# Output norm of the difference attention: factors in one go, applied where the output projection reads its rows

## Chip, cores and metric

The kernel runs on one core of a Trainium2 chip, as one launch. The metric is the device time of a launch in microseconds (us); lower is better. The engines are named PE (TensorE), DVE (VectorE), ACT (ScalarE), POOL (GpSimd) and SP (SyncE, which issues the DMAs).

## What is computed

A transformer layer (difference attention and dilated attention side by side, then a gated output) and a second layer with sliding-window attention, on 2048 tokens of width 1024 in float32. The part that matters here:

```python
dq, dk, dv, bq, bk, bv, z = jnp.split(u, IN_SPLIT_IDX, axis=-1)
...
a = diff_attention(dq, dk, dv, lam, diff_slopes)      # (B, S, 4 heads, 128)
a = rms_norm(a, diff_sub_norm_g[i]) * (1.0 - lam_init)
a = a.reshape(B, S, DIFF_WIDTH)
...
b = dilated_attention(bq, bk, bv, dil_slopes).reshape(B, S, DIL_WIDTH)
y = jnp.concatenate([a, b], axis=-1) * jax.nn.silu(z)
x = x + y @ w_out[i]
```

The norm runs over the 128 columns of one head. So each row of each head has one factor, `1 / sqrt(mean(a * a) + eps)`: 2048 tokens times 4 heads, 8192 factors in all.

## The kernel before

Six stages follow one another in the trace, called A, B1, B2, C, D and E here after the functions. They overlap a little, since a scheduler sets the order of the instructions on each engine from a simulated timeline.

- **A** (0 to 773 us): input projection. It leaves queries, keys, values and `silu(z)` (`sz`) in DRAM.
- **B1** (`phase_b1`, 769 to about 1460 us): difference attention. A step `g` is one head `h` and one tile of 128 queries: 64 steps. Each step has two softmaxes (`e`) of two halves (`hf`) of 1024 keys. `scores` puts a half on PE (4 matmuls, L322); one DVE instruction (L328) evicts it from PSUM, adds the position bias and takes the maximum. `exps` is ACT's (L338). `combine` works out `cc` on DVE (L344, L346) and lets POOL subtract the second softmax from the first (L355, L356). `transposes` (PE L366, ACT L367, DVE L368) and `pv` (PE L380 to L382) follow some steps later.
- `finish` (L390 on) closes a pair of steps. It transposes the output back (L405), ACT divides by the softmax sum (L406) and sums the squares into `ssq` (L408). After every second pair it has four query tiles of a head. Then `rsqrt_dve` (L233) turns the four sums per row into factors: 13 DVE instructions on tiles of 128x4, each of which needs the one before. POOL multiplies the rows by `sz` times gain (L411), ACT scales each of the four tiles by its factor (L413), and SP stores them to `scr["y"][0]` (L414). That is 16 times in B1.
- **B2** (`phase_b2`): dilated attention. POOL splits transposed weights there (L586, L587) and merges the patterns (L659 to L678).
- **C** (`phase_c`): for each of 16 token tiles, `load_y` reads the rows of `y` (L806, 512 columns of the difference attention; L807 and L811, the rest), `product` transposes them (L797) and multiplies by `w_out`. The tile of L806 comes from the pool `c_y0` of one buffer, so the next load waits until PE has transposed the last one. The weights are split into high and low parts on POOL and DVE (L755).
- **D**, **E**: the second layer.

The factor loop, and the code that calls it:

```python
for step in range(3):
    nc.vector.tensor_mul(a, y, y)
    nc.vector.tensor_mul(a, a, v)
    if step < 2:
        nc.vector.scalar_tensor_tensor(y, a, (3.0, 12.0)[step], y, ALU.subtract, ALU.mult)
...
if half == 1:
    rs = rsqrt_dve(nc, fp, ssq, 128)
    nc.gpsimd.tensor_mul(an, an, szt)
    for t in range(4):
        nc.scalar.activation(an[:, t], an[:, t], AF.Copy, scale=rs[:, t:t + 1])
```

Of the kernel before, what the change touches and what calls it, by code (L numbers as in the profile page):

```python
# [7 lines left out]
F32 = mybir.dt.float32  # L8
F32R = mybir.dt.float32r
I32 = mybir.dt.int32  # L10
AF = mybir.ActivationFunctionType
# [5 lines left out]
P = 128  # L17
# [5 lines left out]


def rsqrt_mean(nc, c, pool, ss, n, out=None):
    """1 / sqrt(ss / n + eps), refined by one Newton step."""
    w = ss.shape[-1]
    sd = pool.tile([P, w], F32, name="rm_sd")
    nc.scalar.activation(sd, ss, AF.Sqrt, bias=c["eps"], scale=1.0 / n)
    v = pool.tile([P, w], F32, name="rm_v")  # L30
    nc.vector.tensor_scalar(v, ss, 1.0 / n, EPS, ALU.mult, ALU.add)
    nc.vector.reciprocal(sd, sd)
    nc.vector.tensor_mul(v, v, sd)
    nc.vector.tensor_mul(v, v, sd)
    nc.vector.tensor_scalar(v, v, -0.5, 1.5, ALU.mult, ALU.add)
    if out is None:
        out = pool.tile([P, w], F32, name="rm_o")
    nc.vector.tensor_mul(out, sd, v)
    return out
# [191 lines left out]


def rsqrt_dve(nc, pool, ss, n, out=None):  # L233
    """1 / sqrt(ss / n + eps) on VectorE alone: exponent-halving start, three Newton steps (the
    first leaves -2 y, the second 16 y, and the third takes the factor out)."""
    w = ss.shape[-1]
    v = pool.tile([P, w], F32, name="rd_v")
    nc.vector.tensor_scalar(v, ss, 1.0 / n, EPS, ALU.mult, ALU.add)
    sh = pool.tile([P, w], I32, name="rd_i")
    nc.vector.tensor_scalar(sh, v.bitcast(I32), 1, None, ALU.logical_shift_right)  # L240
    y = pool.tile([P, w], F32, name="rd_y")
    nc.vector.tensor_scalar(y.bitcast(I32), sh, -1.0, float(0x5F3759DF), ALU.mult, ALU.add)
    a = pool.tile([P, w], F32, name="rd_a")
    if out is None:
        out = y
    for step in range(3):
        if w == 1:
            nc.vector.tensor_scalar(a, v, y, y, ALU.mult, ALU.mult)
        else:
# [4 lines that stand above are left out]
        else:  # L254
            nc.vector.tensor_scalar(a, a, -0.5 / 4096, 1.5 / 16, ALU.mult, ALU.add)
            nc.vector.tensor_mul(out, y, a)
    return out


def phase_b1(tc, c, scr, ndist, sub_g, lam):  # L260
    nc = tc.nc
    NQ = 4 * NT
    with (
# [11 lines left out]
        tc.tile_pool(name="b_v", bufs=5) as vp,  # L275
        tc.tile_pool(name="b_p", bufs=6) as pp,
        tc.tile_pool(name="b_o", bufs=2) as op,
        tc.tile_pool(name="b_f", bufs=8) as fp,
        tc.tile_pool(name="b_pt", bufs=3, space=PSUM) as ps_t,
        tc.tile_pool(name="b_po", bufs=1, space=PSUM) as ps_o,  # L280
        tc.tile_pool(name="b_ps", bufs=2, space=PSUM) as ps_s,
# [102 lines left out]
        def evacuate(p):  # L384
            ot = op.tile([P, 256], F32, name="b_ot")
            nc.scalar.activation(ot, outs.pop(p), AF.Copy)
            outs[p, "t"] = ot

        def finish(p):
            h, pr = divmod(p, 8)  # L390
            b, half = divmod(pr, 2)
            if half == 0:
                outs["an"] = op.tile([P, 4, 128], F32, name="b_an")
                outs["ssq"] = fp.tile([P, 4], F32, name="b_ssq", bufs=2)
                szt = op.tile([P, 4, 128], F32, name="b_sz")
                nc.sync.dma_start(
                    szt, scr["sz"][b * 512:(b + 1) * 512, h * 128:(h + 1) * 128].rearrange("(t p) w -> p t w", p=P))
                nc.gpsimd.tensor_mul(szt, szt, g08.unsqueeze(1).broadcast_to([P, 4, 128]))
                outs["sz"] = szt
            an, ssq, szt = outs["an"], outs["ssq"], outs["sz"]  # L400
            ot = outs.pop((p, "t"))
            pb = ps_t.tile([P, 4, P], F32, name="t_ps")
            for qi in range(2):
                t = 2 * half + qi
                nc.tensor.transpose(pb[:, qi], ot[:, qi * P:(qi + 1) * P], c["id"])  # L405
                nc.scalar.activation(an[:, t], pb[:, qi], AF.Copy, scale=st[2 * p + qi]["r0"])  # L406
                junk = op.tile([P, P], F32, name="b_j")
                nc.scalar.activation(junk, an[:, t], AF.Square, accum_out=ssq[:, t:t + 1])  # L408
            if half == 1:
                rs = rsqrt_dve(nc, fp, ssq, 128)  # L410
                nc.gpsimd.tensor_mul(an, an, szt)  # L411
                for t in range(4):
                    nc.scalar.activation(an[:, t], an[:, t], AF.Copy, scale=rs[:, t:t + 1])  # L413
                nc.sync.dma_start(  # L414
                    scr["y"][0][b * 512:(b + 1) * 512, h * 128:(h + 1) * 128].rearrange("(t p) w -> p t w", p=P), an)

# [4 lines left out]
        for g in range(NQ + LT + 5):  # L421
            h, qt = divmod(g, NT)
            if g < NQ and qt == 0:
                for j in range(4):
                    load_v(h, j)
            if g < NQ and qt % 4 == 1:
                ng = g + 3
                if ng < NQ:
                    load_q(ng // NT, (ng % NT) // 4)
            for s in range(4):  # L430
                e, hf = divmod(s, 2)
                if g < NQ:
                    with tc.high_priority(offset=AHEAD) if g < EARLY else nullcontext():
                        scores(g, e, hf)
                    if qt == NT - 1 and h < 3 and hf == 1:
                        for j in range(4):
                            load_k(h + 1, e, j)
                if 0 <= g - LT < NQ:
                    transposes(g - LT, s)
                p, half = divmod(g - LT - 2, 2)  # L440
                if 0 <= p < NQ // 2:
                    for kt in range(8 * half + 2 * s, 8 * half + 2 * s + 2):
                        pv(p, kt)
                if s == FIN and half == 0 and 0 <= p - 1 < NQ // 2:
                    finish(p - 1)
                if g < NQ and hf == 1:
                    with tc.high_priority(offset=AHEAD) if g < EARLY else nullcontext():
                        exps(g, e)
            if g < NQ:
                with tc.high_priority(offset=AHEAD) if g < EARLY else nullcontext():  # L450
                    combine(g)
            p, half = divmod(g - LT - 2, 2)
            if half == 1 and 0 <= p < NQ // 2:
                evacuate(p)


LB = 4
# [309 lines left out]
def phase_c(tc, c, scr, x, p, w_out, ple_g, w_gate, w_proj, norm_g):  # L767
    nc = tc.nc
    with (
# [20 lines left out]
            store[k, ch] = w  # L790

        def to_t(src_of, dst, cuts):
            """transpose 128-column pieces, cuts[i]:cuts[i + 1] at a time, and split them into dst[:, 0] and dst[:, 1]"""
            for b, m in zip(cuts, [e - b for b, e in zip(cuts, cuts[1:])]):
                ps = pt.tile([P, 4, P], F32, name="c_tp")
                for j in range(m):
# [6 lines left out]
        def load_y(t):  # L803
            rows = slice(t * P, (t + 1) * P)
            ys = [yp.tile([P, 512], F32, name="c_yn") for yp in (yp0, yp1)]
            nc.sync.dma_start(ys[0], scr["y"][0][rows])  # L806
            nc.sync.dma_start(ys[1][:, 0:384], scr["y"][1][rows])  # L807
            state["y", t] = ys

# [1 line left out]
            nc.sync.dma_start(state["y", t][1][:, 384:512], scr["y"][2][t * P:(t + 1) * P])  # L811

        def product(t, cuts):
            """y times wo, of the 128-column pieces from cuts[0] to cuts[-1]"""
            ys = state["y", t]
            if cuts[0] == 0:
                state["yt", t] = (ap_.tile([P, 2, KD, P], F32R, name="c_at"),
# [96 lines left out]


def prep_swa(tc, c, scr, table, onehot, sinks, pm):
    """Sink logits, and the position bias by distance, repeated by rows so that a pitch one short reads it as a
    Toeplitz tile. All in units of 1/8."""
    nc = tc.nc
    sk8 = c["const"].tile([P, 16], F32, name="e_sk")  # L920
    nc.sync.dma_start(sk8, sinks.broadcast_to([P, 16]))
# [310 lines left out]
def consts(tc, cp):  # L1232
# [3 lines left out]
    make_identity(nc, c["id"])  # L1236
    c["eps"] = cp.tile([P, 1], F32, name="eps")
    nc.vector.memset(c["eps"], EPS)
    c["qs_dq"] = cp.tile([P, 8], F32, name="qs_dq")
    c["qs_bq"] = cp.tile([P, 8], F32, name="qs_bq")  # L1240
    for h in range(8):
# [3 lines left out]


def diff_lambda(tc, c, lams):
    nc, cp = tc.nc, c["const"]
    lt = cp.tile([P, 4, 64], F32, name="lt")
    for i, ap in enumerate(lams):  # L1250
        nc.sync.dma_start(lt[:, i], ap.broadcast_to([P, 64]))
    pr = cp.tile([P, 2, 64], F32, name="lpr")
    for i in range(2):
        nc.vector.tensor_mul(pr[:, i], lt[:, 2 * i], lt[:, 2 * i + 1])
    s2 = cp.tile([P, 2], F32, name="ls2")
    nc.vector.reduce_sum(s2, pr, axis=AX.X)
    nc.scalar.activation(s2, s2, AF.Exp)
    c["lam"] = cp.tile([P, 1], F32, name="lam")
    nc.vector.tensor_sub(c["lam"], s2[:, 0:1], s2[:, 1:2])
    nc.vector.tensor_scalar(c["lam"], c["lam"], LAM_INIT, None, ALU.add)  # L1260


def tables():
# [65 lines left out]
```

## Time and profile before

| | |
|---|---|
| median of 3 runs | 3122.9 us (3122.07 to 3132.4) |
| profiled execution, first to last instruction | 3126.1 us |
| PE busy | 96% of the span |
| DVE / ACT / POOL busy | 63% / 51% / 37% |
| mean granted PE clock | 0.977 of full speed |
| DMA | 352.78 MB, 112 GB/s over the span |

The profile gives one execution, on the same single core. Of that execution only the span is known, 3.2 us over the median of the runs. "Busy" is the union of an engine's instructions; matmuls are pipelined. The idle time that stands before a group of instructions is put down to what released the engine last.

### The profile page before, as it was taken

The page shows a single profiled execution, that of the slowest core. Times are in us where ns is not written, and L with a number is a line of the kernel's source. Part 1 is how long each engine was busy: PE and PEld are TensorE (multiplying, and loading weights), DVE is VectorE, ACT ScalarE, POOL GpSimd, SP SyncE. Part 2 cuts the span into 40 slices and gives each one's busy share as a digit, 9 for nine tenths or more (in the row PEclk, how much of TensorE's full clock was granted, in tenths as well). Part 3 has the DMA queues.
Part 4 walks back from the last instruction along what each step waited for, and adds up shares of the span by engine and source line. Part 5 has one row for each costly group of instructions (what it writes and reads, how often), then busy time and mean ns, then how long its engine had stood idle before and what let it go on. Part 6 is the DMA issues. An engine that isn't in the chain of part 4 may idle for free.

```text
span 3126.1 us, 45716 instructions
## 1 busy us (share of the span) xinstructions
PE 2988.1 (96%) x15778; PEld 2499.6 (80%) x15778; DVE 1980.9 (63%) x4986; ACT 1591.5 (51%) x3528; POOL 1165.9 (37%) x1052
## 2 busy tenths in 40 slices
PE   8999999999988888988999989999999999999998
PEld 7788888887877777777887867888888888888787
DVE  4215555423999999997787765444445666666765
ACT  5223233312877666776877753222235666666621
POOL 1110011110876667763454540000035565555421
PEclk9999999999999999998999999999999999999999
DMA  7654444415131211106757563233273424232452
GB/s 211 126 132 102 104 118 118 111 61 174 30 91 39 81 55 48 54 15 154 173 143 163 123 167 112 88 107 105 89 238 97 155 88 155 88 116 80 130 190 84
DMA packets 421928, 352.78 MB, mean 113 GB/s; under 512 B 104480, under 2 KB 367168, under 8 KB 418624
## 3 DMA queue, kind: packets, MB, share of 16 engines
q1 hardware_dynamic: 421552, 348.83, 39.8%
q8 instruction: 126, 2.06, 0.3%
q0 software_dynamic: 144, 1.02, 0.2%
q14 instruction: 106, 0.87, 0.1%
HBM read 234.26 MB, written 116.52 MB: 112 GB/s over the span
## 4 chain that ended last, share of the span: by engine, by line
PE 80%; DVE 11%; DMA 4%; issue 2%; ACT 2%; SPq 1%; POOL 0%; DVEq 0%; ACTq 0%; POOLq 0%
PE psm L181 7%; PE psm L183 7%; PE psm L182 7%; PE e_mm L762 5%; PE e_mm L764 5%; PE s_ps L322 5%; PE e_mm L763 4%; PE c_mm L762 4%; PE c_mm L763 4%; PE c_mm L764 4%; DVE et L328 4%; PE d_sr L564 4%; PE t_ps L366 2%; PE f_mm L762 2%; PE f_mm L763 2%
## 5 line engine op out<-in xcount | busy, mean ns | idle before, releaser
L181 PE MATMUL psm<-w,hh 128*128 128x512 f32 x1024 | 406.3, 398 | 9.9 <-DVE t L111 7.1
L183 PE MATMUL psm<-w,hh 128*128 128x512 f32 x1024 | 399.5, 393 | 0.0
L182 PE MATMUL psm<-w,hl 128*128 128x512 f32 x1024 | 399.3, 391 | 0.0
L982 POOL TENSOR_TENSOR e_wt<-e_raw,e_wt 128x1024 fp32r<-128x1024 f32 x80 | 191.3, 2398 | 478.1 <-DMA e_raw<-in_a_w_in_dram 403.9
L322 PE MATMUL s_ps<-kst,qst 128*128 128x512 f32 x1024 | 309.3, 429 | 55.2 <-DVE mx L328 54.6
L101 POOL TENSOR_TENSOR w<-wraw,w 128x512 fp32r<-128x512 f32 x64 | 81.6, 1297 | 599.6 <-ACT w L100 589.6
L356 POOL TENSOR_TENSOR et<-et 128x1024 f32<-128x1024 f32 x124 | 295.1, 2401 | 0.0
L322 PEld LDWEIGHTS s_ps<-kst,qst 128*128 128x128 f32 x1024 | 187.3, 202 | 103.7 <-DVE mx L328 77.1
L338 ACT ACTIVATE et<-et,nm 128x2048 f32<-128x2048 f32 x128 | 257.0, 2007 | 5.7
L181 PEld LDWEIGHTS psm<-w,hh 128*128 128x128 f32 x1024 | 193.3, 189 | 48.5 <-DVE t L111 7.5
L762 PE MATMUL e_mm<-e_x,e_wt 128*128 128x512 f32 x576 | 228.1, 396 | 1.3 <-DVE e_k L1024 0.9
L764 PE MATMUL e_mm<-e_x,e_wt 128*128 128x512 f32 x576 | 226.8, 394 | 0.0
L763 PE MATMUL e_mm<-e_x,e_wt 128*128 128x512 f32 x576 | 226.6, 393 | 0.0
L183 PEld LDWEIGHTS psm<-w,hh 128*128 128x128 f32 x1024 | 192.9, 189 | 41.1
L182 PEld LDWEIGHTS psm<-w,hl 128*128 128x128 f32 x1024 | 193.7, 189 | 38.3
L355 POOL TENSOR_SCALAR et<-et,cc 128x1024 f32<-128x1024 f32 x124 | 138.4, 1131 | 215.8 <-DVE cc L346 122.9
L366 PE MATMUL t_ps<-id,et 128*128 128x128 f32 x1024 | 163.2, 289 | 21.0 <-DVE ptl L368 19.8
L1070 DVE CUSTOM_DVE_ANT_0 e_es<-e_s,e_bias,e_sk 128x256 f32<-128x256 f32 (+1 forms) x256 | 117.3, 472 | 104.1 <-PE e_s L1062 73.5
L1083 POOL TENSOR_SCALAR e_es<-e_es,e_l 128x256 f32<-128x256 f32 (+1 forms) x256 | 119.6, 488 | 170.2 <-DVE e_l L1081 105.2
L367 ACT ACTIVATE pth<-t_ps 128x512 fp32r<-128x512 f32 x256 | 146.4, 590 | 62.8 <-PE t_ps L366 57.7
L368 DVE TENSOR_TENSOR ptl<-t_ps,pth 128x512 fp32r<-128x512 f32 x256 | 170.5, 681 | 12.0 <-ACT pth L367 11.6
L328 DVE CUSTOM_DVE_ANT_0 et<-s_ps,nd,mx 128x1024 f32<-128x1024 f32 x128 | 163.5, 1277 | 19.9 <-PE s_ps L322 18.3
(265 smaller groups left out, 7936.6 us busy)
## 6 DMA issues: line engine op xcount, KB each, us to landing
e_raw<-in_a_w_in_dram SPq DMA_DIRECT2D x80, 512.0 KB, 3.6
wraw<-in_w_in_dram SPq DMA_DIRECT2D x64, 256.0 KB, 3.4
kst<-s_dk SPq DMA_DIRECT2D x128, 128.0 KB, 3.8
d_k<-s_bk SPq DMA_DIRECT2D x32, 512.0 KB, 12.0
s_xt<-c_at SPq DMA_DIRECT2D x32, 512.0 KB, 6.5
e_x<-s_xt SPq DMA_DIRECT2D x32, 512.0 KB, 6.9
t<-in_x_dram SPq DMA_DIRECT2D x32, 256.0 KB, 5.4
s_dv<-t SPq DMA_DIRECT2D x32, 256.0 KB, 3.1
```

What stands on the lines that cost most here:

```text
L181: nc.tensor.matmul(ps, ah, cur[k][:, 0], start=k == 0, stop=False)
L182: nc.tensor.matmul(ps, al, cur[k][:, 0], start=False, stop=False)
L183: nc.tensor.matmul(ps, ah, cur[k][:, 1], start=False, stop=k == KD - 1)
L322: nc.tensor.matmul(ps[:, b * 512:b * 512 + 512], lhs, heads[h, "k", e, i, 2 * hf + b], start=i == 0, stop=i == 1)
L328: nc.vector.tensor_tensor_reduce(et[:, hf], ps, bias[:, off:off + 1024], 1.0, -3.0e38 if hf == 0 else mx[:, 0:1], ALU.add, ALU.max, mx[:, ...
L338: nc.scalar.activation(ev, ev, AF.Exp, bias=nm, scale=slope, accum_out=st[g]["l"][:, e:e + 1])
L356: nc.gpsimd.tensor_sub(es[0][:, hf], es[0][:, hf], es[1][:, hf])
L366: nc.tensor.transpose(pt[:, j], src[:, (4 * (kg % 2) + j) * P:(4 * (kg % 2) + j + 1) * P], c["id"])
L762: nc.tensor.matmul(ps, ah, bh, start=first, stop=False)
L763: nc.tensor.matmul(ps, al, bh, start=False, stop=False)
L764: nc.tensor.matmul(ps, ah, bl, start=False, stop=last)
L982: nc.gpsimd.tensor_sub(w[:, 1], raw, w[:, 0].bitcast(F32))
```

## The change

The sums of squares of all heads and tiles go to one constant tile, `ssq_sub`, of 128 rows x 4 heads x 16 tiles. `finish` no longer calls `rsqrt_dve` and no longer scales: what it stores in `scr["y"][0]` lacks the factor. After the last step of B1, one `rsqrt_dve` turns the whole tile (128x64) into factors, in place. In C, `load_y` has POOL multiply the 512 loaded columns by the four factors of each row. Besides, the pool of the factor loop has 2 buffers instead of 8, and the scratch tiles of `diff_lambda` lie in a pool of their own that is closed after use.

```diff
@@ phase_b1
-        tc.tile_pool(name="b_f", bufs=8) as fp,
+        tc.tile_pool(name="b_f", bufs=2) as fp,
@@ finish
-                outs["ssq"] = fp.tile([P, 4], F32, name="b_ssq", bufs=2)
...
-                nc.scalar.activation(junk, an[:, t], AF.Square, accum_out=ssq[:, t:t + 1])
+                nc.scalar.activation(junk, an[:, t], AF.Square, accum_out=c["ssq"][:, h, 4 * b + t:4 * b + t + 1])
             if half == 1:
-                rs = rsqrt_dve(nc, fp, ssq, 128)
                 nc.gpsimd.tensor_mul(an, an, szt)
-                for t in range(4):
-                    nc.scalar.activation(an[:, t], an[:, t], AF.Copy, scale=rs[:, t:t + 1])
@@ end of phase_b1
+        ssq = c["ssq"].rearrange("p h t -> p (h t)")
+        rsqrt_dve(nc, fp, ssq, 128, ssq)
@@ phase_c, load_y
             nc.sync.dma_start(ys[0], scr["y"][0][rows])
+            yv = ys[0].rearrange("p (h w) -> p h w", h=4)
+            nc.gpsimd.tensor_mul(yv, yv, c["ssq"][:, :, t:t + 1].broadcast_to([P, 4, 128]))
@@ consts
+    c["ssq"] = cp.tile([P, 4, NT], F32, name="ssq_sub")
@@ diff_lambda
-    nc, cp = tc.nc, c["const"]
+    nc = tc.nc
+    c["lam"] = c["const"].tile([P, 1], F32, name="lam")
+    with tc.tile_pool(name="l_c", bufs=1) as cp:
```

The scheduler moves instructions with it. On DVE, around the 15th step of B1, the order before was this (`rd_*` are the tiles of the factor loop, `et` and `s_ps` those of L328, `ptl` that of L368):

```order
L251 TENSOR_TENSOR rd_a<-rd_a,rd_v 128x4
L368 TENSOR_TENSOR ptl<-t_ps,pth 128x4x128
L253 SCALAR_TENSOR_TENSOR rd_y<-rd_a,rd_y 128x4
L250 TENSOR_TENSOR rd_a<-rd_y 128x4
L251 TENSOR_TENSOR rd_a<-rd_a,rd_v 128x4
L344 RECIPROCAL r_7968<-l 128x2
L253 SCALAR_TENSOR_TENSOR rd_y<-rd_a,rd_y 128x4
L346 TENSOR_SCALAR cc<-r_7968,l,lam 128x1
```

and now, at the same step:

```order
L328 ISA et,mx<-s_ps,nd 128x1024
L328 ISA mx 128x1
L344 RECIPROCAL r_7929<-l 128x2
L346 TENSOR_SCALAR cc<-r_7929,l,lam 128x1
L328 ISA et,mx<-s_ps,nd,mx 128x1024
L328 ISA mx 128x1
L368 TENSOR_TENSOR ptl<-t_ps,pth 128x4x128
```

No instruction of the factor loop is left in B1's steps; the one set of 13 (128x64) stands in B2, spread over its first softmaxes.

On SP, where B2's first keys (`d_k`) are loaded, a store of B1 stood in between before (L516, L414, L519; after the change these lines are L514, L410, L517):

```order
-L516 DMA d_q<-s_bq 128x2048
-L414 DMA s_y_137<-b_an 128x4x128
-L519 DMA d_k_14057<-s_bk 64x2048 x2
+L514 DMA d_q<-s_bq 128x2048
+L517 DMA d_k_13727<-s_bk 64x2048 x2
```

That store now stands earlier in the queue or behind B2's loads.

On POOL, at the start of C, the new multiplies (L806 after the change) stand like this (L753 is the split of `w_out`, L657 and L660 are work of B2):

```order
L806 TENSOR_TENSOR c_yn<-c_yn,ssq_sub 128x512
L753 TENSOR_TENSOR c_wo_0_18941<-c_raw,c_wo_0_18941 128x512
L657 TENSOR_TENSOR d_o_17284<-d_o_17284,d_d_18288 128x512 x2
```

```order
L806 TENSOR_TENSOR c_yn<-c_yn,ssq_sub 128x512
L660 TENSOR_TENSOR d_sd<-d_sz,d_d_18797 128x1024
L753 TENSOR_TENSOR c_wo_1_18981<-c_raw,c_wo_1_18981 128x512
L806 TENSOR_TENSOR c_yn<-c_yn,ssq_sub 128x512
L753 TENSOR_TENSOR c_wo_1_18991<-c_raw,c_wo_1_18991 128x512
```

The first three multiplies stand among the last merges of B2 and the weight splits; the other 13 follow behind the splits, ahead of stage D's.

## Rows read from the trace of the kernel before

**Rows 1.** Chain that ended last, 772 to 1430 us, by line (cut by the view).

```profile
by line: PE s_ps L322 20.9%; DVE et L328 17.4%; PE t_ps L366 9.5%; DVE ptl L368 7.2%; issue 7.0%; PE o_ps L380 5.1%; PE o_ps L381 5.1%; PE o_ps L382 5.0%; DVE rd_a L250 4.0%; DVE rd_a L251 3.2%; DVE rd_a L255 2.9%; DVE rd_y L242 2.4%; DVE r
```

**Rows 2.** Busy time by stretch: stretch, length, PE, PEld, DVE, ACT, POOL, clock, DMA.

```profile
801.32:845.28 43.96, 43.96 (x298) 39.22 (x297) 38.64 (x70) 36.04 (x64) 41.80 (x23) 1.00 0.05 13
845.28:1421.91 576.63, 502.50 (x3056) 433.71 (x3054) 539.48 (x932) 404.99 (x777) 402.59 (x240) 0.92 0.18 53
```

**Rows 3.** The same stretches, L328 alone: DVE busy (evictions and read-outs), clock, DMA.

```profile
801.32:845.28 43.96, 25.15 (x40) 1.00 0.05 13
845.28:1421.91 576.63, 266.10 (x426) 0.92 0.18 53
```

**Rows 4.** PE groups, 845.28 to 1421.91 us: busy, mean ns, idle before, releaser.

```profile
L322 PE MATMUL s_ps<-kst,qst 128*128 128x512 f32 x856 | 260.5, 431 | 52.3 <-DVE mx L328 51.6
L366 PE MATMUL t_ps<-id,et 128*128 128x128 f32 x852 | 135.7, 287 | 17.1 <-DVE ptl L368 17.1
```

**Rows 5.** DVE groups of the factor loop, 784 to 1440 us.

```profile
L250 DVE TENSOR_TENSOR rd_a<-rd_y 128x4 f32<-128x4 f32 x43 | 30.4, 707 | 0.3
L251 DVE TENSOR_TENSOR rd_a<-rd_a,rd_v 128x4 f32<-128x4 f32 x42 | 23.9, 568 | 0.5
L255 DVE TENSOR_SCALAR rd_a<-rd_a 128x4 f32<-128x4 f32 x14 | 20.2, 1442 | 0.1
L240 DVE TENSOR_SCALAR rd_i<-rd_v 128x4 int32<-128x4 int32 x15 | 19.8, 1319 | 0.0
...
L242 DVE TENSOR_SCALAR rd_y<-rd_i 128x4 int32<-128x4 int32 x15 | 17.4, 1162 | 0.0
...
L253 DVE SCALAR_TENSOR_TENSOR rd_y<-rd_a,rd_y 128x4 f32<-128x4 f32 x28 | 16.7, 598 | 0.1
L238 DVE TENSOR_SCALAR rd_v<-b_ssq 128x4 f32<-128x4 f32 x15 | 12.3, 823 | 0.5 <-ACT b_j L408 0.5
...
L256 DVE TENSOR_TENSOR rd_y<-rd_y,rd_a 128x4 f32<-128x4 f32 x14 | 8.7, 623 | 0.0
```

**Rows 6.** Timeline of DVE, then POOL, 898 to 902 us: start, length.

```profile
898.62 2.30 DVE L250 TENSOR_TENSOR rd_a<-rd_y 128x4 f32<-128x4 f32 x1
...
901.42 0.15 DVE L250 TENSOR_TENSOR rd_a<-rd_y 128x4 f32<-128x4 f32 x1
...
898.51 2.40 POOL L356 TENSOR_TENSOR et<-et 128x1024 f32<-128x1024 f32 x1
```

**Rows 7.** Groups of the whole execution: ACT's scaling, POOL's multiply by `sz`.

```profile
L411 POOL TENSOR_TENSOR b_an<-b_an,b_sz 128x512 f32<-128x512 f32 x16 | 20.8, 1300 | 20.5 <-ACT b_j L408 20.5
...
L413 ACT ACTIVATE b_an<-b_an,rd_y 128x128 f32<-128x128 f32 x64 | 20.4, 390 | 6.1 <-DVE rd_y L256 6.1
```

**Rows 8.** Timeline of SP at B2's first loads.

```profile
1425.83 0.38 SPq L414 DMA_DIRECT2D s_y<-b_an  x1
1426.26 2.32 SPq L519 DMA_DIRECT2D d_k<-s_bk  x2
```

**Rows 9.** Busy time by stretch, C's steady part (columns as rows 2).

```profile
1880.00:2320.00 440.00, 433.53 (x2056) 354.37 (x2055) 203.71 (x588) 129.89 (x276) 11.92 (x5) 1.00 0.37 118
```

**Rows 10.** The tile of the `y` rows, 1960 to 2040 us.

```profile
L806 SPq DMA_DIRECT2D c_yn<-s_y x3: 358/382/383, 1977.1 to 2033.8; - x3
...
DMA to landing us min/median/max: 3.1/4.6/6.6
```

**Rows 11.** Timelines of SP, POOL and PE at the start of C.

```profile
1829.65 0.33 SPq L806 DMA_DIRECT2D c_yn<-s_y  x1
...
1843.95 0.32 SPq L806 DMA_DIRECT2D c_yn<-s_y  x1
...
1843.18 1.91 POOL L662 TENSOR_TENSOR d_sd<-d_sz,d_d 128x1024 f32<-128x1024 f32 x1 [15.02 <-DVE d_d L653]
...
1849.02 2.19 POOL L755 TENSOR_TENSOR c_wo<-c_raw,c_wo 128x512 fp32r<-128x512 f32 x1 [2.25 <-ACT c_wo L754]
...
1842.41 0.87 PE L797 MATMUL c_tp<-id,c_yn 128*128 128x128 f32 x4
```

More of the change, by code (lines that the diff above doesn't have):

```diff
@@ L399, in finish @@
                 outs["sz"] = szt
-            an, ssq, szt = outs["an"], outs["ssq"], outs["sz"]
+            an, szt = outs["an"], outs["sz"]
             ot = outs.pop((p, "t"))
@@ L1247, in diff_lambda @@
 def diff_lambda(tc, c, lams):
-    nc, cp = tc.nc, c["const"]
[L1249 to L1260, printed above, removed]
+    nc = tc.nc
+    c["lam"] = c["const"].tile([P, 1], F32, name="lam")
+    with tc.tile_pool(name="l_c", bufs=1) as cp:
+        lt = cp.tile([P, 4, 64], F32, name="lt")
+        for i, ap in enumerate(lams):
+            nc.sync.dma_start(lt[:, i], ap.broadcast_to([P, 64]))
+        pr = cp.tile([P, 2, 64], F32, name="lpr")
+        for i in range(2):
+            nc.vector.tensor_mul(pr[:, i], lt[:, 2 * i], lt[:, 2 * i + 1])
+        s2 = cp.tile([P, 2], F32, name="ls2")
+        nc.vector.reduce_sum(s2, pr, axis=AX.X)
+        nc.scalar.activation(s2, s2, AF.Exp)
+        nc.vector.tensor_sub(c["lam"], s2[:, 0:1], s2[:, 1:2])
+        nc.vector.tensor_scalar(c["lam"], c["lam"], LAM_INIT, None, ALU.add)
 def tables():
```

## The prediction

> **What bounds the kernel now.** The chain of waits comes first: it says which instructions the end hangs on while B1 runs. There PE's matmuls alternate with DVE's evictions, as one would think, but four kinds of DVE instruction on tiles of 128x4 alone hold 4.0, 3.2, 2.9 and 2.4% [rows 1]. Those are links of the factor loop: tiny work, on the path.
>
> Next come the busy times by stretch [rows 2], one before the first factor loop (801.32 to 845.28 us) and one from the first to near the end of B1 (845.28 to 1421.91). In the first, PE is busy 43.96 of 43.96 us at full clock. In the second it is busy 502.50 of 576.63 at a mean clock of 0.92, while DVE is busy 539.48. So the bound changes from PE to DVE when the loops begin. How many steps lie in each is read from L328, which gives four evictions and four read-outs a step: 40 and 426 instructions [rows 3], 5 and 53.25 steps. That is 8.79 us a step without loops and 10.83 with them.
>
> Third, who keeps PE waiting in the second stretch: before the score matmuls 52.3 us, before the transposes 17.1 us, both ended by DVE [rows 4]. The evictions behind which PE waits stand in DVE's queue behind the loop's instructions.
>
> Last, why the loop is dear. Its eight groups sum to 30.4 + 23.9 + 20.2 + 19.8 + 17.4 + 16.7 + 12.3 + 8.7 = 149.4 us in 186 instructions [rows 5], 0.80 us each on four elements a partition. One and the same L250 takes 0.15 us at 901.42 but 2.30 at 898.62, where it ends at 900.92, just when the POOL instruction that began at 898.51 and took 2.40 ends [rows 6]. So it is held until POOL is done. At 0.15 the 186 would take 28 us; the other 121 are waiting, and the evictions behind wait too.
>
> **The change part by part.**
>
> *The loops leave B1.* 13 instructions per loop, 14 loops in the second stretch. The price of the stretch after that is bounded from PE. Upper end of the gain: PE never idles and runs at full clock. Its 298 matmuls in 43.96 us are 147.5 ns each; 3056 of them are 450.8 us, 126 less than 576.6 [rows 2]. Lower end: the two waits go and nothing else, 52.3 + 17.1 = 69 us [rows 4]. In between, the pace of the clean stretch: 53.25 steps at 8.79 us are 468 us, a gain of 108. I take 108, because the clean stretch is the same code with the loop taken away. What would be late next: DVE without its share of the loops is 540 less about 139, 401 us or 7.5 a step; POOL 402.59 / 53.25 = 7.6; ACT 404.99 / 53.25 = 7.6, less what follows. All are under 8.79, so PE sets the pace, with DVE and POOL not far behind, which is why I don't take the floor of 126.
>
> *ACT's scaling goes.* 64 instructions at 390 ns are 25 us by that mean, 20.4 us of busy union [rows 7]. ACT is at 405 of 577 us [rows 2]; worth nothing by itself.
>
> *The last store no longer stands in front of B2's keys.* L414 waited for the last step of its loop and stood between B2's first query load and the key loads; it held SP from 1425.83 to 1426.26 [rows 8]. B2's start waits for the keys. Gain 0 to 2, I take 1: the queue is passed once, and what lets the loads begin otherwise stays.
>
> *One loop of 128x64 in B2.* The 13 wide instructions were not in the trace. Lower bound 0.15 us each, 2 us; upper bound 2.30 each, 30 us [rows 6]. The sixteenth loop before also fell in B2, so the difference is at most 28 us of DVE time; no one needs the factors before C's first multiply, hundreds of us later. The cover is that stretch; without it, up to 28. I take 0.
>
> *16 multiplies on POOL in C.* The nearest row is the multiply by `sz`, same shape, 1.30 us [rows 7]; together 21 us of POOL. POOL is busy 11.92 of 440 us in C's steady part [rows 9]. There a load is issued each (2033.8 - 1977.1) / 2 = 28.4 us, right after the buffer is free, and lands after 4.6, at most 6.6 us [rows 10]. Load and multiply take 5.9 to 7.9 of 28.4, so the steady tiles cost 0. At the start there is less room. The second tile's load is issued at 1829.65, lands by 1836.3 at the latest, and is multiplied by 1837.6; PE wants it at 1842.41, and POOL was idle 15.02 us until 1843.18 [rows 11]: hidden. The third's load is issued at 1843.95, so its multiply ends between 1848.4 (3.1 us to land) and 1851.9; behind it in POOL's queue stands the weight split that began at 1849.02 [rows 11]. That is late by 0 to 2.9 us, and the weights of `w_out` are waited for. I take 1.
>
> Here a rule speaks against the change. The trace shows that a small DVE instruction is held while POOL runs one [rows 6], and C gets 16 new POOL instructions. The Trainium skill, page SBUF — State Buffer, section Who interferes with whom, says that a DVE instruction with two inputs in SBUF cannot run beside a GpSimd one that reads SBUF, and waits for its end. By it each multiply could hold DVE once; at the 1.30 us of the row [rows 7] that is 21 us of DVE in C. By the rows DVE is busy 203.71 of 440 us there and PE 433.53 [rows 9], so I put none of it on the path; with all of it on the path the sum would end at 3036.
>
> *The scratch of `diff_lambda`.* Its loads and a small table's now follow one another in the same memory in the first 40 us, and two weight loads pass the table's load on SP. Both serve later work; 0.
>
> **The sum.** 3126.1 - 108 - 1 + 1 = 3018 us by the profiled span, which is 3.2 over the median; so **3015 us** for the median, 108 under 3122.9. With the bounds: at best 126 and 2, 2995; at worst 69 gained and 5 lost in C and at the edges, 3059.
>
> **The rivals.** A measurement of this kernel can tell about 0.3%, 9 us, from no change.
>
> *PE's clock stays down.* Of the 126 us over the floor, 74 are idle (576.63 - 502.50) and 52 are matmuls that ran slower than in the clean stretch (502.50 - 450.8) [rows 2]. If the idle shrinks as forecast, to 468 - 451 = 17 us, but the clock stays at 0.92 between its two levels of 1.2 and 2.4 GHz, because short waits go on, the gain is only 57: 3066, or 3058 if more of the idle goes. For it: DVE is at 88% and POOL at 95% of the clean stretch, so small waits are likely. Against: in that stretch the clock was 1.00 all the same. The Trainium skill, page TensorE: Matmul & The Clock Gate, section What's actually happening, has the clock follow how busy PE has been; by that rule the loss goes away with the idle.
>
> *DVE is held up in C.* The mechanism and price are above: 16 times 1.30, ending at 3036.
>
> *Nothing is gained.* DVE spends the time of the loops waiting for PE anyway. Then the evictions start when they did, and the time is within 9 us of 3122.9. Against it: PE's idle time is ended by DVE, not the reverse [rows 4].
>
> *Slower: C's loads come onto the path.* One buffer holds the rows, so load and multiply follow PE's transposes. If the scheduler's order made PE want the next tile at once, each of 16 tiles would add up to 6.6 + 1.3 = 7.9 us [rows 7, 10], 126 in all: 3015 + 126 = 3141. It decides once each tile waits over (108 + 9) / 16 = 7.3 us. Against it: PE wants the tile 28.4 us later.
>
> **How the numbers follow.** The forecast, PE at or near the clean pace in B1 (gain 90 to 126): 0.74. The clock stays down: 0.15. DVE held up in C: 0.03. Nothing gained: 0.04. Slower: 0.04. Faster by over 0.3%: 0.74 + 0.15 + 0.03 = 0.92; the same 0.04; slower 0.04. The range, 2995 to 3059, is that of the bounds and takes in the upper half of the clock's rival.
>
> **What would show it.** In the profile after: no factor loop among B1's steps; the stretch of 53.25 steps takes about 468 us, at a clock near 1.00, with PE's waits for DVE before L322 and L366 under 20 us together instead of 69; DVE near 85% of it. The multiplies in C take about 1.3 us each and no transposes of the rows wait for POOL. B2, D and E keep their lengths within 3 us. The forecast is wrong if the pace stays over 9.5 us a step, if POOL or ACT ends PE's waits, or if C grows by over 5 us.

## The result, and the profile after

The changed kernel takes **3013.2 us** (median of 4 runs, 3008.3 to 3018.9). Against the kernel before, on the same chip, the ratio is **0.9639** (95% interval 0.9619 to 0.9658), about 110 us less. The forecast was 3015, range 2995 to 3059. One execution of the kernel before was disturbed (6304.0 us) and is left out of the ratio. The profiled execution took 3018.9 us with a span of 3017.1, against the span of 3126.1 before.

Where the time went is read first from landmarks, the starts of the same instructions in both traces (us from the start of the span):

| landmark | before | after | difference |
|---|---|---|---|
| first score eviction of B1 (L328) | 744.7 | 745.5 | +0.8 |
| last value matmul of B1 (L381) | 1455.5 | 1343.2 | -112.3 |
| first eviction of B2 (`d_en`) | 1447.0 | 1332.6 | -114.4 |
| first residual eviction of C (L836) | 1872.3 | 1762.5 | -109.8 |
| last residual eviction of C (L836) | 2273.7 | 2165.2 | -108.5 |
| end of the span | 3126.1 | 3017.1 | -109.0 |

So all of it is made in B1, 4.6 us are given back between the first eviction of B2 and that of C, and C, D and E keep their lengths within 2 us. Now B1. The busy time by stretch, as [rows 2]: stretch, length, then busy time and count of PE, PEld, DVE, ACT and POOL, the granted clock, DMA share and GB/s.

```profile
801.30:845.30 44.00, 44.00 (x297) 39.23 (x297) 38.51 (x72) 35.33 (x64) 41.69 (x24) 1.00 0.05 13
845.30:1321.09 475.79, 470.52 (x3131) 415.86 (x3130) 418.90 (x780) 391.57 (x739) 405.11 (x241) 1.00 0.25 71
```

And L328 alone in the second stretch, as [rows 3]: DVE's busy time, its count of evictions and read-outs, the clock.

```profile
845.30:1321.09 475.79, 267.15 (x432) 1.00 0.25 71
```

The 432 at eight a step are 54 steps. The stretch runs on for 6 us behind the last of them, as the line of the 216 read-outs shows (min/median/max ns, first and last start):

```profile
L328 DVE DVE_READ_ACCUMULATOR2_ANT mx<- x216: 75/82/88, 847.0 to 1315.0; 128x1 f32 x108
```

Up to its end, at 1315.05, the 54 steps take 469.75 us, which is 8.70 a step (8.81 if the 6 us are counted too). It was 10.83 with the loops, over a stretch that was cut where an eviction begins, and 8.79 in the stretch of before that had none. The clock of the stretch rose from 0.92 to 1.00. PE is busy 470.5 of 475.8 us, DVE 418.9: the bound is PE again. Who waits for whom is in the groups of that stretch, as [rows 4]: busy time, mean ns of one, idle time of the engine before them and what ended it.

```profile
L322 PE MATMUL s_ps<-kst,qst 128*128 128x512 f32 x860 | 242.0, 405 | 1.8 <-DMA kst<-s_dk 1.2 <-DVE mx L328 0.6
L366 PE MATMUL t_ps<-id,et 128*128 128x128 f32 x884 | 128.1, 272 | 3.0 <-DVE ptl L368 3.0
...
L328 DVE CUSTOM_DVE_ANT_0 et<-s_ps,nd,mx 128x1024 f32<-128x1024 f32 x108 | 138.1, 1279 | 23.4 <-PE s_ps L322 21.9
L328 DVE CUSTOM_DVE_ANT_0 et<-s_ps,nd 128x1024 f32<-128x1024 f32 x108 | 131.6, 1218 | 7.0 <-PE s_ps L322 6.2 <-POOL et L355 0.8
```

The roles are exchanged. PE's waits before L322 and L366 were 52.3 and 17.1 us, and are 1.8 and 3.0; now DVE waits for PE before its evictions, 28.1 us. The score matmul itself went from 431 to 405 ns as the clock rose.

The one factor loop of the attention that is left stands in B2. Its DVE groups between 1352 and 1372 us:

```profile
L253 DVE SCALAR_TENSOR_TENSOR rd_y<-rd_a,rd_y 128x64 f32<-128x64 f32 x2 | 1.4, 698 | 0.0
L251 DVE TENSOR_TENSOR rd_a<-rd_a,rd_v 128x64 f32<-128x64 f32 x3 | 1.0, 341 | 0.0
L238 DVE TENSOR_SCALAR rd_v<-ssq_sub 128x64 f32<-128x64 f32 x1 | 0.7, 746 | 0.0
```

With the five other groups the 13 instructions sum to 4.5 us. The 16 multiplies in C, by the line's own view (durations as min/median/max, first and last start, then what ended POOL's idle time before them):

```profile
L806 POOL TENSOR_TENSOR c_yn<-c_yn,ssq_sub x16: 1049/1052/1173, 1706.7 to 2128.8; 128x512 f32<-128x512 f32 x16
its engine sat idle before it (us, times) until:
  DMA c_yn<-s_y: 365.3, 16
who waited for it (us, times):
```

The list of who waited for it is empty. C's steady part, as [rows 9] (columns as above):

```profile
1771.00:2211.00 440.00, 434.23 (x2061) 355.33 (x2061) 202.90 (x588) 129.51 (x274) 24.53 (x17) 1.00 0.36 118
```

PE and DVE are as busy as before; POOL has the 12 multiplies that fall in this window more, 12 x 1.05 = 12.6 us.

### The profile page after: what moved, and what is told of

Read it like the earlier page. It is cut to its first block, busy times and chain, and to the rows that moved or that the text cites. A ratio compares the mean times of both kernels' runs of the same rounds, so it can differ in the third digit from the quotient of the medians.

```text
span 3017.1 us, 45471 instructions
## 1 busy us (share of the span) xinstructions
PE 2946.5 (98%) x15778; PEld 2471.4 (82%) x15778; DVE 1847.2 (61%) x4791; ACT 1567.9 (52%) x3464; POOL 1184.6 (39%) x1068
## 5 line engine op out<-in xcount | busy, mean ns | idle before, releaser
L356 POOL TENSOR_TENSOR et<-et 128x1024 f32<-128x1024 f32 x124 | 296.1, 2410 | 0.0
L322 PE MATMUL s_ps<-kst,qst 128*128 128x512 f32 x1024 | 290.4, 408 | 4.5 <-DVE mx L328 3.3
L322 PEld LDWEIGHTS s_ps<-kst,qst 128*128 128x128 f32 x1024 | 176.9, 191 | 44.0 <-DVE mx L328 17.4
L368 DVE TENSOR_TENSOR ptl<-t_ps,pth 128x512 fp32r<-128x512 f32 x256 | 168.9, 682 | 19.7 <-ACT pth L367 19.3
L328 DVE CUSTOM_DVE_ANT_0 et<-s_ps,nd,mx 128x1024 f32<-128x1024 f32 x128 | 163.7, 1279 | 26.7 <-PE s_ps L322 24.7
L328 DVE CUSTOM_DVE_ANT_0 et<-s_ps,nd 128x1024 f32<-128x1024 f32 x128 | 156.0, 1218 | 14.0 <-PE s_ps L322 7.6
```

What stands on the lines that cost most here:

```text
L322: nc.tensor.matmul(ps[:, b * 512:b * 512 + 512], lhs, heads[h, "k", e, i, 2 * hf + b], start=i == 0, stop=i == 1)
L328: nc.vector.tensor_tensor_reduce(et[:, hf], ps, bias[:, off:off + 1024], 1.0, -3.0e38 if hf == 0 else mx[:, 0:1], ALU.add, ALU.max, mx[:, ...
L356: nc.gpsimd.tensor_sub(es[0][:, hf], es[0][:, hf], es[1][:, hf])
L368: nc.vector.tensor_sub(tl[:, :, qi], pt, th[:, :, qi].bitcast(F32))
```

## The experiments

The theory: in B1 the loop's small DVE instructions wait for POOL's running instruction, the evictions queued behind them come late, PE waits and its clock falls. Rivals: any 13 instructions in that queue cost as much; ACT's scaling or the store was the cost; the scheduler's new order brought the gain. Ten kernels test this, in three groups. Beside each group the kernel before was run too, with medians of 3124.6, 3127.0 and 3126.4 us (19, 7 and 13 runs); the ratios below are to these. The changed kernel was not run beside them, so a difference to its 3013.2 us is across groups, between which the kernel before moved by up to 4.1 us. The stretch for the runs that are as slow as before is 845.30 to 1421 us.

**The loops put back, nothing else.** (The pool of the loop's tiles gets its 8 buffers back, here and in the other runs with small loops. The chains of reciprocals below ran with 8 as well and were fast, so the buffers are not the cost.)

```diff
             if half == 1:
+                rsqrt_dve(nc, fp, c["ssq"][:, h, 4 * b:4 * b + 4], 128)
                 nc.gpsimd.tensor_mul(an, an, szt)
```

> The changed kernel, with the 16 small loops put back on DVE where they stood in B1 (13 instructions of 128x4 each, their result read by nobody); the rows are still scaled in C, ACT's scaling stays out, and the store still waits for no factor. Theory: the loops alone, held on DVE behind POOL's instructions, cost B1 its 108 us: 3115 to 3125, with the clock near 0.92 again in B1 and the loop's instructions at a mean of 0.7 to 0.9 us. Rival (it was ACT's scaling, the store's place, or the rescheduled order): 3010 to 3030.

Measured: 3129.4 us, ratio to before 1.0013 (0.9999 to 1.0027). The stretch, a PE group in it, and two DVE groups of the loop (784 to 1440 us):

```profile
845.30:1421.00 575.70, 494.50 (x3060) 432.06 (x3059) 531.60 (x929) 382.92 (x724) 402.48 (x240) 0.93 0.19 54
```

```profile
L322 PE MATMUL s_ps<-kst,qst 128*128 128x512 f32 x856 | 257.8, 429 | 59.5 <-DVE mx L328 59.3
```

```profile
L250 DVE TENSOR_TENSOR rd_a<-rd_y 128x4 f32<-128x4 f32 x42 | 41.8, 994 | 0.8
...
L238 DVE TENSOR_SCALAR rd_v<-ssq_sub 128x4 f32<-128x4 f32 x14 | 18.0, 1288 | 0.0
```

The whole loss is back, 4 us beyond the range expected, with the clock at 0.93 and DVE busy for 531.6 us, although ACT's scaling and the store's wait are still gone. The loops alone cost it.

**The same without POOL's combination.** The loops stay; in `combine` POOL does nothing.

```diff
             for hf in range(2):
-                nc.gpsimd.tensor_scalar(es[1][:, hf], es[1][:, hf], cc, 1.0, ALU.mult, ALU.mult)
-                nc.gpsimd.tensor_sub(es[0][:, hf], es[0][:, hf], es[1][:, hf])
+                pass
```

> As the run with the loops back, but POOL's two instructions of the combination (multiply by cc and subtract, 128x1024 each) are left out, so the second map's weights are not subtracted; the loops stay on DVE, same count and same forms. Theory: without POOL's instructions nothing holds the loop's, they take 0.15 to 0.2 us each, and the time is that of the changed kernel or a little less: 3000 to 3020. Rival (the loop costs by itself, by its count or as a chain): 3100 to 3125.

Measured: 3011.4 us, ratio 0.9633 (0.9608 to 0.9658). The stretch from 845.3 to 1320 us, then the two-input loop groups from 784 to 1440 us:

```profile
845.30:1320.00 474.70, 468.22 (x3127) 415.76 (x3125) 436.52 (x959) 391.52 (x745) 34.49 (x28) 1.00 0.25 67
```

```profile
L251 DVE TENSOR_TENSOR rd_a<-rd_a,rd_v 128x4 f32<-128x4 f32 x48 | 8.5, 176 | 0.5
L250 DVE TENSOR_TENSOR rd_a<-rd_y 128x4 f32<-128x4 f32 x48 | 8.3, 172 | 0.6
```

The same instructions, L250's, take 172 instead of 994 ns once POOL runs little beside them (34.5 us in the stretch instead of 402.5), and the same 16 loops cost nothing that can be measured. Neither their count nor their being a chain is the price. Without POOL's work the loop would have been harmless; without the loop POOL's work is.

**Three chains of 13 instructions, one form each,** in those 16 places, in the changed kernel. The one with reciprocals is:

```diff
             if half == 1:
+                rv = fp.tile([P, 4], F32, name="rd_v")
+                nc.vector.reciprocal(rv, c["ssq"][:, h, 4 * b:4 * b + 4])
+                for _ in range(12):
+                    nc.vector.reciprocal(rv, rv)
                 nc.gpsimd.tensor_mul(an, an, szt)
```

The second has `nc.vector.tensor_scalar(rv, rv, 1.0, 1.0, ALU.mult, ALU.add)` in the loop, the third `nc.vector.tensor_sub(rv, rv, sq)` with `sq` the four sums.

> The changed kernel, with 13 reciprocals of 128x4 on DVE in each of those 16 places, a chain like the loop's, in place of its 13 instructions. In the trace of before, the reciprocal of 128x2 beside POOL's instructions took 0.16 us, while the loop's forms took 0.57 to 1.44. Theory (the cost is the wait for POOL, not the count of instructions): 13 x 14 x 0.16 = 29 us of DVE in B1, which the idle of DVE after the change covers: 3010 to 3025. Rival (any 13 small instructions in DVE's queue cost the 108): 3110 to 3125. Its numbers are not used by anyone.

> As the run with the 13 reciprocals, but 13 one-input tensor_scalar instructions with two constants (128x4, the form of L238 and L255) in each of the 16 places; nobody reads them. Theory: this form waits for POOL's running instruction as the loop's did (rows of before: 0.82 to 1.44 us), so 13 x 0.8 to 1.0 us each time and 3100 to 3135, mean over 0.6 us. Rival (only instructions with two inputs in SBUF are held; the one-input ones in the loop waited for the link before them): 0.15 us each, 3010 to 3025.

> The same with 13 two-input tensor_tensor instructions (128x4, the form of L250, both inputs in SBUF). Theory: held as in the loop (rows of before: 0.57 to 0.71 us), 3090 to 3130, mean over 0.5 us. Rival (only the one-input forms are held): 0.15 us each, 3010 to 3025.

Measured: reciprocals 3015.8 us, ratio 0.9647 (0.9623 to 0.9672); one-input `tensor_scalar` 3138.3, ratio 1.0039 (1.0024 to 1.0054); two-input `tensor_tensor` 3122.4, ratio 0.9988 (0.9975 to 1.0001). The line of the 12 repeated instructions in each of the three (min/median/max ns):

```profile
L412 DVE RECIPROCAL rd_v<-rd_v x192: 152/173/180, 849.7 to 1375.6; 128x4 f32<-128x4 f32 x192
```

```profile
L412 DVE TENSOR_SCALAR rd_v<-rd_v x192: 144/170/2439, 848.3 to 1487.9; 128x4 f32<-128x4 f32 x192
```

```profile
L413 DVE TENSOR_TENSOR rd_v<-rd_v,ssq_sub x192: 135/162/2427, 850.1 to 1486.3; 128x4 f32<-128x4 f32 x192
```

The medians are alike; the maxima are not. That also closes the rival of the order: of DVE's 788 instructions from B1's first eviction to near its last, at least 760 stand in the same order, by kind, in the run with reciprocals and in that with `tensor_scalar`, and yet the times lie some 120 us apart. The rivals by form fall too: the one-input and the two-input form are both dear. The one-input one came out 3 us beyond its range. Each form runs in under 0.2 us when it runs freely. The second and third are held for up to 2.4 us, which is what one POOL subtraction takes (2412 ns mean for L356 in the changed kernel's B1), and the reciprocal never: 142 of its 192 begin and end while one and the same POOL instruction runs, against one of the 192 in either of the other two. No chain reads anything that POOL writes, so this is no wait for data. In the stretch that makes a mean of 783 ns for the one and 172 for the other:

```profile
L412 DVE TENSOR_SCALAR rd_v<-rd_v 128x4 f32<-128x4 f32 x168 | 131.5, 783 | 2.5
```

```profile
L412 DVE RECIPROCAL rd_v<-rd_v 128x4 f32<-128x4 f32 x168 | 28.9, 172 | 2.0
```

PE's side of it, the stretch and then its wait before the scores, first with reciprocals and then with `tensor_scalar`:

```profile
845.30:1320.00 474.70, 467.13 (x3091) 411.81 (x3089) 426.74 (x946) 389.90 (x737) 403.63 (x240) 1.00 0.24 68
L322 PE MATMUL s_ps<-kst,qst 128*128 128x512 f32 x856 | 242.6, 406 | 4.3 <-DMA kst<-s_dk 2.8 <-DVE mx L328 0.7
```

```profile
845.30:1421.00 575.70, 491.98 (x3050) 429.90 (x3049) 535.10 (x929) 381.29 (x720) 402.25 (x240) 0.92 0.19 54
L322 PE MATMUL s_ps<-kst,qst 128*128 128x512 f32 x853 | 259.2, 432 | 62.2 <-DVE mx L328 62.1
```

The hold can be seen one instruction at a time. Timelines of DVE, then POOL, in the run with one-input `tensor_scalar` (start, length; x2 and x3 are neighbours drawn together):

```profile
897.38 1.26 DVE L412 TENSOR_SCALAR rd_v<-rd_v 128x4 f32<-128x4 f32 x1
898.56 0.68 DVE L368 TENSOR_TENSOR ptl<-t_ps,pth 128x512 fp32r<-128x512 f32 x1
899.16 1.80 DVE L412 TENSOR_SCALAR rd_v<-rd_v 128x4 f32<-128x4 f32 x1
...
902.02 0.57 DVE L412 TENSOR_SCALAR rd_v<-rd_v 128x4 f32<-128x4 f32 x3
```

```profile
896.22 4.72 POOL L356 TENSOR_TENSOR et<-et 128x1024 f32<-128x1024 f32 x2
903.14 2.21 POOL L355 TENSOR_SCALAR et<-et,cc 128x1024 f32<-128x1024 f32 x2 [2.20 <-DVE rd_v L412]
```

POOL's two subtractions run from 896.22 to 900.94, the first for about half of it, to some 898.6. DVE's instruction of 897.38 ends at 898.64, that of 899.16 at 900.96: each just after one of POOL's. At 902.02 POOL is idle, and three of them take 0.57 us. Between the first two, L368 ran in its usual 0.68 us while POOL was busy; one of its two inputs (`t_ps`) lies in PSUM.

The Trainium skill, page SBUF — State Buffer, section Who interferes with whom, has a DVE instruction contend with GpSimd in two cases: with two inputs in SBUF, when GpSimd's instruction reads SBUF, or in a mode that uses both of DVE's port pairs, which `tensor_scalar` can enter. The two maxima of 2427 and 2439 ns agree with the two cases. The section also says that an instruction with at most one SBUF input, outside those modes, does not contend. The reciprocal's 180 ns agree with that if it has no such mode; it is not among the forms that the section lists.

**A quarter of the loops.** One per head, 128x16 wide.

```diff
             if half == 1:
+                if b == 3:
+                    rsqrt_dve(nc, fp, c["ssq"][:, h], 128)
                 nc.gpsimd.tensor_mul(an, an, szt)
```

> The changed kernel with a quarter of the loops put back on DVE: one per head, 128x16 wide, 13 instructions each, after the head's last rows; their result is read by nobody. Theory A (each loop delays the evictions queued behind it, whatever idle time DVE has elsewhere): 108 x 4 / 16 = 27 us more, 3033 to 3047. Theory B (a loop costs only when DVE's whole work in the stretch exceeds what PE's pace allows; 419 of 476 us are busy after the change, and 4 loops at 13 x 0.8 us are 42): covered, 3008 to 3020.

Measured: 3039.8 us, ratio 0.9723 (0.9707 to 0.9739), 26.7 over the changed kernel. Two PE groups and the dearest of the loop's, 845.3 to 1345 us:

```profile
L322 PE MATMUL s_ps<-kst,qst 128*128 128x512 f32 x856 | 243.5, 409 | 10.3 <-DVE mx L328 8.9 <-DMA kst<-s_dk 1.2
...
L366 PE MATMUL t_ps<-id,et 128*128 128x128 f32 x880 | 127.1, 276 | 7.9 <-DVE ptl L368 7.8
```

```profile
L250 DVE TENSOR_TENSOR rd_a<-rd_y 128x16 f32<-128x16 f32 x9 | 8.5, 941 | 0.1
```

Theory A, cost by the loop. Three loops fall in this stretch (9 instructions of L250 at three a loop), and the loop's eight groups sum to 27.3 us there; the fourth falls in B2. In the profiled execution the last value matmul of B1 (L381) starts at 1366.0 us, 22.8 later than in the changed kernel, so most of the 26.7 is B1's. DVE is idle for some 60 us of the stretch, and the loops are not hidden all the same. The run with reciprocals gives the other side: 14 chains of 13 x 0.172 = 2.2 us each, 31 us of DVE in all, cost 2.7 us, which can't be told from nothing. So chains of 2 us cost nothing measurable, and chains of 9 cost most of their length. That the buffers between PE and DVE take up the short delays is a likely reason; no run shows it.

**ACT's scaling alone.** The kernel before without it: the factors are worked out and not applied.

```diff
-                for t in range(4):
-                    nc.scalar.activation(an[:, t], an[:, t], AF.Copy, scale=rs[:, t:t + 1])
```

> The kernel before, without ACT's 64 scalings of the rows (the factors are worked out but not applied); the loops stay. Theory: ACT is not on the path in B1, so 3115 to 3127, same as before within 0.3%. Rival (ACT's 25 us and the store behind it were part of the gain): 3095 to 3110.

Measured: 3119.3 us, ratio 0.9981 (0.9966 to 0.9997): 5 us or 0.2%, just apart from nothing. That is as much as the loops put back differ from before on the other side, and the order of B1's work differs a little between all of these kernels. The 110 us are not here.

**The multiplies in C**: left out, moved to DVE, and done four times over.

```diff
-            nc.gpsimd.tensor_mul(yv, yv, c["ssq"][:, :, t:t + 1].broadcast_to([P, 4, 128]))
```
```diff
-            nc.gpsimd.tensor_mul(yv, yv, c["ssq"][:, :, t:t + 1].broadcast_to([P, 4, 128]))
+            nc.vector.tensor_mul(yv, yv, c["ssq"][:, :, t:t + 1].broadcast_to([P, 4, 128]))
```
```diff
-            nc.gpsimd.tensor_mul(yv, yv, c["ssq"][:, :, t:t + 1].broadcast_to([P, 4, 128]))
+            for _ in range(4):
+                nc.gpsimd.tensor_mul(yv, yv, c["ssq"][:, :, t:t + 1].broadcast_to([P, 4, 128]))
```

> The changed kernel without the 16 multiplies in C, so the rows stay unscaled. Theory (load and multiply are over long before PE wants the rows; only the start of C can show it): 3008 to 3016, the first residual eviction of C not over 2 us earlier against the end of B1. Rival (multiplies or their hold on DVE lie on the path): 16 x 1.05 = 17 us less, 2993 to 3000.

> The changed kernel with the 16 multiplies of C on DVE, which is busy for less than half of C. Theory (C is bound by PE, either engine hides them): 3008 to 3018. Rival (the multiply's wait for the load stands in front of C's evictions in DVE's queue, up to 4.6 us a tile): 3030 to 3090.

> The changed kernel with each of the 16 multiplies done four times on POOL, so the rows are scaled by the fourth power. Theory: load and multiplies take 4.6 + 4 x 1.05 = 8.8 of the 28.4 us that a tile has, so the steady part costs nothing and the start of C up to 3 x 3 x 1.05 = 9 us: 3010 to 3022. Rival (POOL's instructions hold DVE, and that reaches PE in C): 48 x 1.05 = 50 us more, 3050 to 3063.

Measured: left out 3013.5 us, ratio 0.9637 (0.9623 to 0.9652); on DVE 3017.1, ratio 0.9652 (0.9636 to 0.9669); four times 3012.8, ratio 0.9636 (0.9620 to 0.9652). C's steady part in the run with four:

```profile
1771.00:2211.00 440.00, 433.68 (x2055) 355.08 (x2056) 201.19 (x581) 128.59 (x271) 63.31 (x54) 1.00 0.37 119
```

POOL's time there rises from 24.53 to 63.31 us while DVE's stays at 201 and PE's at 434. Between no multiplies and 64 of them the time differs by 0.7 us. On DVE the line shows

```profile
L806 DVE TENSOR_TENSOR c_yn<-c_yn,ssq_sub x16: 673/692/1177, 1702.5 to 2124.2; 128x512 f32<-128x512 f32 x16
```

and DVE stood 14.8 us waiting for their loads; the 4 us more than on POOL are too few to be told apart from none.

## Why the prediction was right

*The bound.* "The bound changes from PE to DVE when the loops begin": shown. With the loops back DVE is busy 531.6 of 575.7 us and PE waits 59.5 us before L322; without them DVE waits for PE. PE's two waits are 4.8 us together, under the 20 that were to show it.

*Why the loop is dear.* The forecast split its 149 us into 28 of work and 121 of waiting for POOL, from one pair of rows of L250 [rows 6]. Without POOL's combination the two-input ones take 0.17 us, so the split holds, if a little more is work: 186 x 0.17 = 32. The rows of before could not say whether the count alone would do harm; the reciprocals show that it does not.

*The pace.* Forecast 53.25 steps at 8.79 us; measured 54 at 8.70, and a clock of 1.00. Taking the clean stretch for the price, not the floor of 126 or the waits alone of 69, was the decision that made the number. B1 gave 112 where 108 stood: in the profiled runs its end moved by 112.3 us, and 0.09 us a step over 53.25 steps is about the difference. That five steps near B1's start would price the other 53 to 1% was partly luck; nothing in the rows of before showed it.

*The clock.* The rival with 0.92 fell. It took the clock as something that might stay; in each run it went with PE's idle time: 0.92 to 0.93 in the stretch where all the loops were held, 1.00 in the changed kernel and in the runs with reciprocals or without POOL's combination, and 0.98 with a quarter of the loops.

*The edges.* ACT's scaling was costed at 0; its run gives 5 us, with 1 to 11 inside the interval, so a small share is not excluded. B2's first eviction came 114.4 us earlier and the last value matmul 112.3, so the start overlaps 2.1 us more, where 1 was forecast, from 0 to 2; no run tests whether the store is the cause. B2 was to keep its length within 3 us and did not: from its first eviction to C's, 4.6 us were given back. PE's wait for the key loads there grew from 3.9 to 6.9 us. The rest is not pinned to one line; the length of that stretch lies between 419.7 and 435.4 us over the runs here, with or without the multiplies. So the sum came out right partly because B1's 4 us more and B2's 4.6 less cancel.

*C.* The multiply took 1.05 us, not 1.30, and the start of C cost nothing that a run can show (forecast 1). The rule of the Trainium skill that spoke against the change, page SBUF — State Buffer, section Who interferes with whom, was taken to put up to 21 us on DVE. DVE's busy time in C did not move (203.71 to 202.90), nor with four times as many. The evictions there read PSUM: L836, `c_mm` from PSUM and `c_xt` from SBUF, has 678/691/694 ns after and 680/692/693 before. They have one input in SBUF, so by that rule they are not held; the forecast gave the rival 0.03, and what it lacked was a look at where C's inputs lie. The rival on the slower side, loads on the path, needed 7.3 us of wait a tile; PE waited 0.7 us in all for the rows.

*DVE after.* "Near 85%": 418.9 / 475.8 = 88%. The wide loop, bounded by 2 and 30 us, took 4.5.

## What to carry to other kernels

A tiny instruction's price is read from its maximum beside its median, not from its shape: the same 128x4 instruction took 0.16 us or 2.4, by what POOL was running. A serial chain of such instructions between evictions should be gathered and moved to where its engine does not feed the bound; then one pass over 128x64 costs about as much as half a loop over 128x4 did. And the time of a stretch that lacks the suspect was here the best price for taking it out, 4 us off, where the waits that it ends were 43 us short and the floor of PE 14 us over.

## What the runs showed of the hardware that was not expected

One-input `tensor_scalar` with constants is held as long as two-input `tensor_tensor` (2439 and 2427 ns at most), even on four elements, while a reciprocal of the same size and count stays at 152 to 180 ns. In the changed kernel `tensor_scalar` on 128x1 with pointers for its factors, L346, stays at 259 to 277 ns, and 35 of its 64 begin and end while one POOL instruction runs; whether the pointers or the single element makes the difference, no run separates. And POOL's multiply by a factor broadcast along the row (1.05 us, L806) is shorter than the same shape by a full tile (1.30 us, [rows 7]).
